# The place of the input's quarter sums on VectorE in a two-layer hybrid decoder trunk

## The chip, the cores and the metric

The kernel runs on one core of a Trainium2 chip. A core has a matrix engine (TensorE, PE in the profile), a vector engine (VectorE, DVE), a scalar engine (ScalarE, ACT), a general engine (GpSimd, POOL) and a queue engine for transfers (SyncE, SP). Each engine works through its own list of instructions in the order in which the list was written; the engines wait for each other by semaphores. The metric is the device time of one execution in microseconds (us), the median of several runs. Less is better.

## The reference

The reference computes a trunk of two layers over one sequence of 512 positions with 2048 features. Each layer normalises its input, multiplies it by one combined input projection and feeds three branches: a short gated convolution, a stick-breaking attention of 8 heads, and a gated linear attention (GLA) of 4 heads. The three results, each times its own gate, are joined and go through an output projection into the residual stream.

```python
def _layer(x, norm_g, w_in, conv_w, conv_b, sb_qn_g, sb_kn_g, gla_w_up, gla_b_up, gla_on_g, w_out):
    h = _rmsnorm(x, norm_g).astype(x.dtype)
    proj = h @ w_in
    ...
    y_conv = _short_conv(cv_h, cv_b, cv_c, conv_w, conv_b) * jax.nn.silu(cv_g.astype(f32))
    q = _rmsnorm(sb_q.reshape(b, s, SB_HEADS, SB_HD), sb_qn_g)
    k = _rmsnorm(sb_k.reshape(b, s, SB_HEADS, SB_HD), sb_kn_g)
    ...
    y_sb = _stick_breaking(q, k, v) * jax.nn.silu(sb_g.astype(f32))
    g = jax.nn.log_sigmoid((gl_lr @ gla_w_up + gla_b_up).astype(f32)) / GLA_TAU
    o = _gla(gl_q, gl_k, gl_v, g)
    y_gla = _rmsnorm(o, gla_on_g).reshape(b, s, GLA_W) * jax.nn.silu(gl_g.astype(f32))
    mix = jnp.concatenate([y_conv, y_sb, y_gla], axis=-1).astype(x.dtype)
    return x + mix @ w_out
```

All data are float32. GLA's queries and keys have 256 columns each, its values and its gate 512 each.

## The kernel before

**Two 16-bit parts for one number.** The kernel multiplies in float16. It writes each float32 operand as a high part (rounded) and a low part (what is left) and takes three of the four cross products. ScalarE makes a high part by a copy with a scale, VectorE the low part by a subtraction. The normalised input lies so in two big tiles `xh` and `xl`, transposed, and stays there for a whole layer.

**Weights.** The weights come in 76 groups of 256 columns, 38 for each layer, in the order in which PE uses them. In a layer the order is: GLA values (two groups, `gla v 0` and `gla v 1`, the second with 16 more columns for the decay's low-rank input), GLA queries (`gla q`), GLA keys (`gla k`), GLA gate (`gla gate 0` and `gla gate 1`), then the convolution's and the attention's groups and the output projection. `fetch` (L362) loads a group two ahead of use on POOL's queue into one of two `st` buffers. `squares` sums its squares on ScalarE (L383), POOL adds them over the partitions (`PARTITION_ALL_REDUCE`, L399), and `wscale` makes a power-of-two scale `ws` of that with four small VectorE steps (L402 to L417). Then `whi` makes the high part of each half of the group on ScalarE (L454) and `wlo` the low part on VectorE (L461), into three buffers each. All of this is traced with a high priority.

**Quick groups.** Most groups, from `gla gate 0` on, are multiplied by a scheme with seven products in place of eight on quarters of the two matrices (`project_quick`, matmuls on L793 and L796). For it a group's weights are split into seven sums of quarters (`wsums`: ScalarE L507, VectorE L508 and the additions L527, L529, L532). The input needs four sums of its quarters as well. `sums_of`, called for the input by `xsums`, makes them once for a layer, in two halves `t` of 256 positions. Each half takes twelve VectorE steps, all recorded on L734 since one helper `do` issues them and keeps them in the list `steps`, and four ScalarE copies (L742). The four parts are written to the tile `s` in float16. The scratch tiles have the tags `zw` and `g`, with two buffers each. `project_quick` first multiplies the first quarter of `x` itself, then parts 0, 2 and 3 of the sums, later part 1.

**Who sets the order.** The code is traced in program order, and a scheduler then writes each engine's list by a simulation of the time: of what is ready it takes what has the highest priority, which is the place in the program, except inside `tc.high_priority`. `order(a, b)` adds an edge without a semaphore: `a` comes behind `b` in the schedule. The kernel uses it to steer. The start of the kernel is laid out by hand for VectorE and ScalarE up to `byhand.__exit__`.

**Around the change.** In a layer the values' groups come first (`project_by_token`, matmuls on L843), then a loop over the tags `qT` and `kT` projects GLA's queries and keys (`project_cols`, L701 to L703) and scales each by its largest entry (`V.tensor_reduce` on L1012 and small steps). Right after the queries, at the end of the loop's first pass, the program calls `xsums`. The decay's work (running sums on L984, its exponent steps L976 to L981) stands ahead of the loop, and in the first layer so does `make_masks` (L134 to L144). Behind the loop stand the two gates and GLA's chunk work (L1044 to L1111), for which POOL clears two tiles of tag `zw` (L1064).

The counter `cursor[0]` counts the groups that have been taken by `weights()`; after the projection of the queries it has moved past them, so that `cursor[0] - 1` is the group `gla q` of that layer.

Of the kernel before, what the change touches and what calls it, by code (L numbers as in the profile page):

```python
# [11 lines left out]
ALU = mybir.AluOpType  # L12
# [31 lines left out]
def hybrid_trunk(ctx, tc, x, norm_g, w_in, conv_w, conv_b, sb_qn_g, sb_kn_g,  # L44
                 gla_w_up, gla_b_up, gla_on_g, w_out, out):
    nc = tc.nc
    V, S, G, T = nc.vector, nc.scalar, nc.gpsimd, nc.tensor
# [5 lines left out]
    GW = 256  # L53
# [21 lines left out]
    def sm(n, tag, bufs=None):  # L75
        return small.tile([P, n], F32, tag=tag, name=nm(tag), bufs=bufs or 1 + (tag in TWICE))

    def wk(shape, tag, bufs=None, dt=F32):
        return work.tile(shape, dt, tag=tag, name=nm(tag), bufs=bufs)

    def newbig(tag, shape, dt, side):
        return big.tile(shape, dt, tag=f"big{side}", name=nm(tag))
# [97 lines left out]
    def allmax(src, n, tag):  # L180

        gm = sm(n, tag + "gm")
        G.partition_all_reduce(gm, src, P, RED.absmax)
        return gm

    def pow2(dst, m, lift, tag):

        c = sm(dst.shape[-1], tag + "pc")
        V.tensor_scalar(c, m, 2.0 ** -90, None, ALU.max)
        V.tensor_scalar(c.bitcast(I32), c.bitcast(I32), 0x7F800000, None, ALU.bitwise_and)  # L190
        V.tensor_scalar(dst, c, 2.0 ** lift, None, ALU.mult)
# [3 lines left out]
    def order(a, b):  # L195
        tc.add_manual_dep(a.ins, b.ins.name, mybir.DependencyInfo(
            mybir.DependencyClass.NoSync, mybir.DependencyReason.DATA), reason="order")
# [145 lines left out]
    loaded = {}  # L343
    cursor = [0]

    staged, whole, narrow, peak, scales = {}, {}, {}, {}, {}

    def junk(n):

# [108 lines left out]

    def wlo(i, h):
        wh, wl = loaded[i][0][h]  # L460
        V.scalar_tensor_tensor(wl[:, :, :GW], staged[i][h], scales[i], wh[:, :, :GW], ALU.mult, ALU.subtract)  # L461
        if i in narrow:
            V.scalar_tensor_tensor(wl[:, :, GW:], narrow[i][:, h * HK:(h + 1) * HK, :], scales[i], wh[:, :, GW:],
                                   ALU.mult, ALU.subtract)
# [12 lines left out]
    def parts_of(i, mm):  # L477

        with tc.high_priority():
            order(wscale(i), mm)  # L480
            if i in quick:
                wsums(i)
                return
            for h in range(2):
                whi(i, h)
                wlo(i, h)
# [165 lines left out]
    xlow(0, 0, mix, True)  # L652
    xlow(0, 1, mix, True)
    wlo(0, 0)
    wlo(0, 1)
    xhigh(1, 0, mix)
    xhigh(1, 1, mix)
# [27 lines left out]
    for l in range(depth):  # L685
# [45 lines left out]
        def sums_of(src, parts, room):  # L731

            def do(f, *a):
                steps.append(f(*a))  # L734

            for t in range(2):
                (h11, h12), (h21, h22), (l11, l12), (l21, l22) = (
                    (a[:, q, 0::2, :], a[:, q, 1::2, :]) for a in src for q in (t, t + 2))

                def put(n, a):  # L740
                    hi, lo = (p_[:, t] for p_ in parts[n])
                    S.activation(hi, a, AF.Copy)  # L742
                    do(V.tensor_tensor, lo, a, hi, ALU.subtract)

                e, g, f = room(t)
                do(V.tensor_tensor, f, h22, l22, ALU.add)
                do(V.tensor_tensor, e, h21, f, ALU.subtract)
                do(V.tensor_tensor, e, e, l21, ALU.add)
                do(V.tensor_tensor, g, h11, e, ALU.subtract)
                do(V.tensor_tensor, g, g, l11, ALU.add)  # L750
                put(0, g)
                do(V.tensor_tensor, f, g, f, ALU.subtract)
                put(3, f)
                put(1, e)
                do(V.tensor_tensor, e, h12, g, ALU.subtract)
                do(V.tensor_tensor, e, e, l12, ALU.add)
                put(2, e)
            return parts
# [11 lines left out]
        def xsums():  # L770

            parts = []
            for _ in range(2):
                a = newbig("s", [P, 4, 2, HK, P], F16, 1 - l)
                parts.extend([a[:, 2 * n], a[:, 2 * n + 1]] for n in range(2))
            return sums_of((xh, xl), parts, lambda t: [wk([P, HK, P], tag) for tag in ("zw", "zw", "g")])
# [47 lines left out]
        def project(cols, dst):  # L824

            if cursor[0] not in quick:
                return project_cols() if cols else project_toks(xh, xl)
            y = dst()
            for _, u in project_quick((xh, xl), insums, y, cols):
                pass  # L830
            if cols:
                return [y[:, c, :] for c in range(2)], u
            return [y[:, 2 * b:2 * b + 2, :].rearrange("p a c -> p (a c)") for b in range(2)], u
# [55 lines left out]
        steps = []  # L889
# [81 lines left out]
        for p in range(2):  # L971
# [3 lines left out]
            a = wk([P, seq], "ga")  # L975
# [26 lines left out]
        for tag in ("qT", "kT"):  # L1002
            o = wk([P, 2, seq], tag)
            ps, u = project(True, lambda: o)
            mx = sm(2, "gamx")
            if tag == "kT":
                with tc.high_priority(offset=1 << 20):
                    for c in range(2):
                        S.activation(o[:, c, :], ps[c], AF.Copy)
                ps = [o[:, c, :] for c in range(2)]  # L1010
            for c in range(2):
                V.tensor_reduce(mx[:, c:c + 1], ps[c], AX.X, ALU.max, apply_absolute_value=True)  # L1012
            gm = allmax(mx, 2, "ga")
            m = sm(1, "gam")
            V.tensor_tensor(m, gm[:, 0:1], gm[:, 1:2], ALU.max)
            p2 = sm(1, tag + "p2")
            pow2(p2, m, -14.0, "ga")
            s_ = sm(1, "gas")
            V.reciprocal(s_, p2)
            for c in range(2):  # L1020
                S.activation(o[:, c, :], ps[c], AF.Copy, scale=s_)
            qk.append(o)
            un = sm(1, tag + "un")
            V.tensor_tensor(un, p2, u, ALU.mult)
            qku.append(un)
            if tag == "qT":
                insums = xsums()
        gq, gk = qk
        att_u = sm(1, "attu")
        V.tensor_scalar(att_u, qku[0], qku[1], 0.125, ALU.mult, ALU.mult)  # L1030
# [289 lines left out]
        for j in range(4):  # L1320
# [21 lines left out]
            for n in range(2):  # L1342
# [11 lines left out]
                for b in range(2):  # L1354
# [4 lines left out]
                    for i in range(4):  # L1359
                        cs = slice(i * P, (i + 1) * P)  # L1360
                        a = S.activation(e[:, cs], rb.rearrange("p a c -> p (a c)")[:, cs], AF.Square,
                                         accum_out=sq[:, 8 * n + 4 * b + i:8 * n + 4 * b + i + 1])
# [42 lines left out]
        steps, out_ = [], {}  # L1405
# [74 lines left out]
```

## Time and profile before

| what | value |
|---|---|
| median of 3 runs | 1647.73 us (1642.52 to 1655.6) |
| the profiled execution | 1646.43 us |
| its span in the profile | 1644.6 us |
| granted TensorE clock | 1.00 |
| data moved | 235.97 MB, 143 GB/s mean |
| GLA queries on PE, first layer | from 74.07 us |
| GLA gate 0 on PE, first layer | from 117.66 us |
| GLA gate 0 on PE, second layer | from 924.43 us |

How to read the profile: the page gives the busy time of each engine, the waits and the groups of instructions by line. A row of the timeline has the start in us, the duration in us, the engine, the line, the operation and its tiles (written `out<-in`), the number of instructions merged into the row, and in brackets how long the engine had been idle before it and what ended that. Durations of neighbouring VectorE rows overlap by about 0.1 us, so the time that a step takes from its engine is the distance between starts. A row of the waits has the engine and the waiting instruction, the releasing one, the sum in us, how often, and the longest. The view by stretch gives each engine's busy time with the number of its instructions in brackets. `wl` and `wh` are low and high parts of weights, `s` the input's sums, `x` or `m` the input's own parts (the first and the second layer), `psp` an accumulator of PE.

### The profile page before, as it was taken

The numbers are of one execution on the slowest core, as the hardware profiler recorded it, in microseconds if no ns is written. First come the engines' busy times: TensorE is split into PE (matmuls) and PEld (weight loads), VectorE is DVE, ScalarE is ACT, GpSimd is POOL, SyncE is SP. The second block draws the span as 40 slices with busy tenths as digits, with TensorE's granted clock in tenths as the row PEclk, the third lists the DMA queues.
The fourth block names the chain that finished last, engine by engine and source line by source line (L and its number), as shares of the span: only waits on it lengthen the run. The fifth ranks groups of instructions, "written<-read, shape, count | busy, mean of one in ns | idle before, by whom it ended". The sixth has DMA issues, their size and how long they took to land.

```text
span 1644.6 us, 41938 instructions
## 1 busy us (share of the span) xinstructions
PE 1619.6 (98%) x18058; PEld 1356.1 (82%) x18058; DVE 1433.7 (87%) x2403; ACT 1192.3 (72%) x1763; POOL 270.7 (16%) x300
## 2 busy tenths in 40 slices
PE   8999999999999999999999999999999999999999
PEld 5757768989899967799986668689898989768998
DVE  7989989989898979898699899898988889878893
ACT  7668887977777776756766788788777878666571
POOL 0122021211112121111102111211121212110110
PEclk9999999999999999999999999999999999999999
DMA  7154435477868677544643544546776776894441
GB/s 260 54 129 140 93 118 114 108 160 142 166 149 167 149 167 197 171 155 142 203 120 105 129 116 116 140 83 140 151 157 153 158 158 155 174 196 141 155 155 53
DMA packets 195995, 235.97 MB, mean 143 GB/s; under 512 B 90259, under 2 KB 156125, under 8 KB 195297
## 3 DMA queue, kind: packets, MB, share of 16 engines
q0 software_dynamic: 79072, 178.27, 41.2%
q1 hardware_dynamic: 107728, 45.56, 14.6%
q10 hardware_dynamic: 9008, 9.45, 1.8%
q8 instruction: 141, 2.31, 0.6%
q14 instruction: 46, 0.37, 0.1%
HBM read 179.65 MB, written 14.68 MB: 118 GB/s over the span
## 4 chain that ended last, share of the span: by engine, by line
PE 33%; DVE 10%; ACT 4%; DMA 3%; issue 2%; SPq 0%; POOL 0%; DVEq 0%; ACTq 0%; POOLq 0%
PE psp L796 11%; PE psp L793 6%; PE psp L843 4%; PE psp L714 2%; PE psp L713 2%; PE psp L712 2%; DVE wl L508 2%; PE psp L702 1%; PE psp L701 1%; PE psp L703 1%; DMA m<-mixd 1%; ACT wh L507 1%; ACT junk L383 1%; DMA kT<-raw 1%; DVE wl L461 1%
## 5 line engine op out<-in xcount | busy, mean ns | idle before, releaser
L507 ACT ACTIVATE wh<-st,ws 128x1024 f16<-128x1024 f32 x264 | 293.8, 1144 | 168.3 <-DVE st L527 89.8
L508 DVE SCALAR_TENSOR_TENSOR wl<-st,ws,wh 128x1024 f16<-128x1024 f32 x264 | 332.1, 1280 | 24.0 <-ACT wh L507 23.8
L383 ACT ACTIVATE junk<-st 128x2048 uint8<-128x2048 f32 x150 | 285.5, 1903 | 19.4 <-DMA st<-in_w_out_dram 10.4
L793 PE MATMUL psp<-s,wh 128*128 128x256 f16 x1280 | 217.7, 273 | 0.0
L793 PEld LDWEIGHTS <-wh 128*128 128x128 f16 x1920 | 187.4, 98 | 23.4 <-issue 1.4
L796 PE MATMUL psp<-wh,s 128*128 128x128 f16 x2048 | 177.2, 219 | 0.8 <-issue 0.8
L714 PE MATMUL psp<-wh,m 128*128 128x256 f16 x640 | 174.5, 273 | 3.1 <-DVE m L1195 3.1
L793 PE MATMUL psp<-s,wl 128*128 128x256 f16 x640 | 174.3, 273 | 0.9 <-DVE wl L508 0.9
L712 PE MATMUL psp<-wh,m 128*128 128x256 f16 x640 | 174.5, 273 | 0.0
L713 PE MATMUL psp<-wl,m 128*128 128x256 f16 x640 | 174.5, 273 | 0.0
L796 PEld LDWEIGHTS <-s 128*128 128x128 f16 x3072 | 172.9, 98 | 1.2 <-issue 1.2
L796 PE MATMUL psp<-wl,s 128*128 128x128 f16 x1024 | 173.3, 219 | 0.0
L461 DVE SCALAR_TENSOR_TENSOR wl<-st,ws,wh 128x2048 f16<-128x2048 f32 x64 | 149.4, 2347 | 16.2 <-ACT wh L454 15.6
L362 POOL DMA_DIRECT2D st<-in_w_in_dram x114 | 110.9, 1051 | 256.0 <-DVE w7l L508 112.7
L454 ACT ACTIVATE wh<-st,ws 128x2048 f16<-128x2048 f32 x62 | 122.4, 1995 | 32.3 <-DVE ws L415 19.2
L796 PEld LDWEIGHTS <-m 128*128 128x128 f16 x2304 | 131.0, 98 | 2.5 <-issue 2.1
L399 POOL PARTITION_ALL_REDUCE wgm<-wm x75 | 55.6, 742 | 456.9 <-ACT junk L383 442.8
L386 POOL DMA_DIRECT2D st<-st x36 | 57.3, 1591 | 356.0 <-ACT junk L383 336.7
L793 PEld LDWEIGHTS <-wl 128*128 128x128 f16 x960 | 93.9, 98 | 13.2 <-DVE wl L508 1.4
L796 PE MATMUL psp<-wh,m 128*128 128x128 f16 x1024 | 91.5, 219 | 0.7 <-DVE ws L415 0.4
L796 PE MATMUL psp<-wl,m 128*128 128x128 f16 x512 | 87.5, 219 | 0.0
L843 PEld LDWEIGHTS <-m 128*128 128x128 f16 x768 | 75.0, 98 | 12.4 <-DMA m<-th 1.3
(443 smaller groups left out, 4136.8 us busy)
## 6 DMA issues: line engine op xcount, KB each, us to landing
st<-in_w_in_dram POOLq DMA_DIRECT2D x114, 1024.0 KB, 8.4
st<-in_w_out_dram POOLq DMA_DIRECT2D x32, 1024.0 KB, 9.3
st<-st POOLq DMA_DIRECT2D x36, 512.0 KB, 6.7
st<-in_w_in_dram SPq DMA_DIRECT2D x6, 1024.0 KB, 12.0
mixd<-g POOLq DMA_DIRECT2D x20, 256.0 KB, 8.0
x<-in_x_dram SPq DMA_DIRECT2D x4, 1024.0 KB, 4.9
qT<-in_x_dram ACTq DMA_DIRECT2D x8, 512.0 KB, 6.8
qT<-xs ACTq DMA_DIRECT2D x8, 512.0 KB, 4.0
```

The costliest lines, as they stand in the source:

```text
L362: load = queue.dma_start(s_, src[l, h * HK * P:(h + 1) * HK * P, c0:c0 + GW].rearrange("(k p) n -> p k n", p=P), max_dma_last_dim=1024)
L383: sq = S.activation(junk(HK * GW).rearrange("p (k n) -> p k n", k=part.shape[1]), part, AF.Square, accum_out=peak[i][:, h:h + 1])
L454: hi = S.activation(wh[:, :, :GW], staged[i][h], AF.Copy, scale=scales[i])
L461: V.scalar_tensor_tensor(wl[:, :, :GW], staged[i][h], scales[i], wh[:, :, :GW], ALU.mult, ALU.subtract)
L507: hi = S.activation(h_, b, AF.Copy, scale=sc)
L508: V.scalar_tensor_tensor(l_, b, sc, h_, ALU.mult, ALU.subtract)
L712: T.matmul(o, ah[:, t, k, :], wh[:, kk, :n], start=st_, stop=False, skip_group_check=True)
L713: T.matmul(o, ah[:, t, k, :], wl[:, kk, :n], start=False, stop=False, skip_group_check=True)
L714: return T.matmul(o, al[:, t, k, :], wh[:, kk, :n], start=False, stop=en, skip_group_check=True)
L793: mm = T.matmul(o, w[q_][:, kk, :], a[p_][:, :, kk, :], start=st_, stop=en, skip_group_check=True)
L796: mm = T.matmul(o[:, t * P:(t + 1) * P], a[p_][:, t, kk, :], w[q_][:, kk, :], start=st_, stop=en, skip_group_check=True)
L843: mm = T.matmul(o[:, :n], a_[:, t, k, :], w[k // HK][part][:, k % HK, :n], start=i == 0 and k == 0, stop=i == 2 and k == KT - 1)
```

## The change

`wlo` keeps its last VectorE instruction for each group in a new dictionary `lows`; as it is called for the two halves of a group in turn, what stays is the low part of the second half. After `xsums`, all 24 VectorE steps of the sums are ordered behind the low part of the second half of `gla q`. The list `steps` is set up anew in each layer, so it holds the sums of that layer alone at this place. The edge has no semaphore and works within VectorE; ScalarE's copies follow by their data. Nothing is computed in another way.

```diff
-    staged, whole, narrow, peak, scales = {}, {}, {}, {}, {}
+    staged, whole, narrow, peak, scales, lows = {}, {}, {}, {}, {}, {}
...
     def wlo(i, h):
         wh, wl = loaded[i][0][h]
-        V.scalar_tensor_tensor(wl[:, :, :GW], staged[i][h], scales[i], wh[:, :, :GW], ALU.mult, ALU.subtract)
+        lows[i] = V.scalar_tensor_tensor(wl[:, :, :GW], staged[i][h], scales[i], wh[:, :, :GW], ALU.mult, ALU.subtract)
         if i in narrow:
...
             if tag == "qT":
                 insums = xsums()
+                for a in steps:
+                    order(a, lows[cursor[0] - 1])
         gq, gk = qk
```

## The prediction

> **What bounds the kernel now.** I read the head of the page first, then the waits of TensorE (PE), then the busy time of each engine by stretch around the edit, then VectorE's (DVE) and PE's timeline there.
>
> ```profile
> span 1644.6 us, 41938 instructions
> PE 1619.6 (98%) x18058; PEld 1356.1 (82%) x18058; DVE 1433.7 (87%) x2403; ACT 1192.3 (72%) x1763; POOL 270.7 (16%) x300
> ```
>
> PE is idle for 1644.6 - 1619.6 = 25.0 us of the whole span. No change of order on DVE can give more than that, and 1% (about what a measurement of this kernel can tell from no change) is 16.5 us. Where does PE wait near the edit? These are its waits between 40 and 121 us; between 852 and 927 us, the same place in the second layer, the view has none.
>
> ```profile
> PE psp L703 <- DVE wl L461: 1.3, 1, 1.3
> PE psp L843 <- ACT wh L456: 0.6, 1, 0.6
> PE psp L843 <- DVE kpc L190: 0.6, 1, 0.6
> ```
>
> The busy time by stretch (columns: stretch, its length, then busy us and instruction count of PE, weight loads, DVE, ACT, POOL, then granted clock, DMA share, GB/s):
>
> ```profile
> 40.00:76.00 36.00, 33.40 (x289) 28.03 (x287) 35.74 (x64) 25.26 (x32) 4.84 (x5) 1.00 0.20 62
> 852.00:885.00 33.00, 33.00 (x281) 27.32 (x280) 32.97 (x44) 22.01 (x26) 2.61 (x4) 1.00 0.21 67
> 80.57:122.79 42.22, 42.22 (x223) 21.49 (x222) 34.96 (x81) 27.80 (x33) 12.46 (x12) 1.00 0.54 125
> 884.47:929.56 45.09, 45.09 (x237) 22.80 (x236) 35.57 (x74) 31.04 (x37) 13.15 (x12) 1.00 0.51 117
> 120.28:240.00 119.72, 119.28 (x1074) 87.20 (x1072) 110.53 (x205) 98.53 (x149) 18.46 (x21) 1.00 0.43 119
> 927.05:1040.00 112.95, 112.51 (x1043) 84.14 (x1041) 103.73 (x195) 94.15 (x143) 18.44 (x21) 1.00 0.46 126
> ```
>
> In the first two rows DVE is full; PE is idle 2.6 us in the first layer and not at all in the second. In the next two, where the edit sends work, DVE has 42.22 - 34.96 = 7.3 us and 45.09 - 35.57 = 9.5 us free. PE binds everywhere here; DVE matters only where PE must wait for it.
>
> **What the change moves.** Nothing is added or removed. Each layer has 24 VectorE steps of the input's sums (all on L734; 12 for each of two halves). Those that stand ahead of the last low part of the query weights must now stand behind it. The sums' busy time ahead of that low part, and the rows of DVE that mark the places:
>
> ```profile
> 40.00:78.30 38.30, 23.77 (x20) 1.00 0.19 58
> 852.00:882.20 30.20, 20.05 (x17) 1.00 0.23 73
> ...
> 44.53 1.22 DVE L734 TENSOR_TENSOR zw<-x,zw 128x1024 f32<-128x1024 f16 x1
> 46.98 0.14 DVE L190 TENSOR_SCALAR kpc<-kpc 128x1 int32<-128x1 int32 x1
> 71.11 1.21 DVE L734 TENSOR_TENSOR s<-zw,s 128x1024 f16<-128x1024 f32 x1
> 72.25 1.21 DVE L734 TENSOR_TENSOR zw<-zw,x 128x1024 f32<-128x1024 f32 x1
> 73.60 2.33 DVE L461 SCALAR_TENSOR_TENSOR wl<-st,ws,wh 128x2048 f16<-128x2048 f32 x1
> 78.30 2.33 DVE L461 SCALAR_TENSOR_TENSOR wl<-st,ws,wh 128x2048 f16<-128x2048 f32 x1
> 882.21 2.33 DVE L461 SCALAR_TENSOR_TENSOR wl<-st,ws,wh 128x2048 f16<-128x2048 f32 x1
> ```
>
> So 20 of 24 steps move in the first layer (their tie is the low part at 78.30) and 17 in the second (882.21). Start to start a step takes 72.25 - 71.11 = 1.14 us: 22.8 us and 19.4 us of DVE work. The ACT copies that feed the low halves of the sums (L742) go with them; ACT has over 14 us free in each receiving stretch, so I cost them at nothing; were ACT full they would delay the sums one for one.
>
> **What it can give.** In the first layer the low part at 73.60 starts late because DVE is full, and PE waits for it:
>
> ```profile
> 69.94 3.88 ACT L454 ACTIVATE wh<-st,ws 128x2048 f16<-128x2048 f32 x2
> ...
> 75.99 0.39 PE L703 MATMUL psp<-x,wl 128*128 128x512 f16 x1 [1.32 <-DVE wl L461]
> ```
>
> Both high parts lie between 69.94 and 73.82. With DVE free the low parts can run at about 71.9 and 74.2 and be done by 76.5 rather than 80.57, 4.1 us sooner, and the 1.3 us go. The wait of 0.6 us for L190 is behind sums on DVE too (44.53 ahead of 46.98 above), so I count it: 1.9 us. The 0.6 us for the ACT high part is the open one: from 0 (its scale is late for another reason) to 0.6. Gain 1.3 to 2.6 us, taken as 1.9. What is late next there is PE itself. The second layer gives 0, since PE has no wait to lose.
>
> On this bound a rule of the Trainium skill can be weighed. It says (Perfetto Trace Analysis, Identifying the Most-Contended Engine) that matmul busy time is no measure of how near TensorE is to its limit, and that the weight-load share is. By weight loads the stretch from 40 to 76 us has 36.00 - 28.03 = 8.0 us of room, and with a gain of that size the sum below would be about 1642.5 us; by the idle rows it is at most 2.6 us. I go by idle time, because a matmul stream without gaps can't be made denser by another order on DVE.
>
> **What it can cost.** The sums have a last moment. The first gate projection of the linear attention reads them; PE runs its first product from x, then three products of 24 matmuls each from s:
>
> ```profile
> 120.28 0.27 PE L793 MATMUL psp<-s,wh 128*128 128x256 f16 x1
> 128.14 0.27 PE L793 MATMUL psp<-x,wh 128*128 128x256 f16 x1
> 927.05 0.27 PE L793 MATMUL psp<-s,wh 128*128 128x256 f16 x1
> ```
>
> (128.14 - 120.28) / 3 = 2.62 us a product. The second of them reads part 2, whose low half is the last step of all: it must be there by 122.9 us and 929.7 us. Up to there 22.8 us must go into 7.3 us of free DVE time in the first layer, and 19.4 into 9.5 in the second: 15.5 and 9.9 us too much, if nothing gives way. What gives way, from these rows:
>
> ```profile
> 85.98 0.31 DVE L962 CAST qT<-lr 128x48 bf16<-128x48 f32 x2
> 87.66 0.29 DVE L962 CAST qT<-lr 128x32 bf16<-128x32 f32 x2
> 92.18 0.69 DVE L969 CAST e<-psm 128x512 bf16<-128x512 f32 x1 [0.58 <-PE psm L965]
> 96.46 2.93 DVE L141 TENSOR_SCALAR masks<-e 128x256 uint8<-128x256 f32 x7
> 102.75 0.42 DVE L1078 TENSOR_TENSOR e<-raw 128x256 f32<-128x256 f32 x1
> 107.03 0.76 DVE L1087 SCALAR_TENSOR_TENSOR e<-e,qT 128x256 f32<-128x256 f32 x2 [1.41 <-ACT qT L1021]
> 108.74 0.75 DVE L1050 TENSOR_TENSOR th<-e,th 128x256 f16<-128x256 f32 x2
> 110.69 0.66 DVE L1012 TENSOR_REDUCE gamx<-kT 128x1 f32<-128x512 f32 x1
> 118.62 4.87 DVE L508 SCALAR_TENSOR_TENSOR wl<-st,ws,wh 128x1024 f16<-128x1024 f32 x4 [1.17 <-ACT wh L507]
> ```
>
> First, the start 4.1 us sooner (first layer only). Second, the chunk work of the linear attention, which the code emits after the sums: L1078 and L1079 (four of about 0.34 from start to start), L1087, L1050, L1012, together about 3.4 us. Third, the small steps of the decay's low-rank input, which the sums delay today: six groups between 85.98 and 87.66, about 1.6 us, can run sooner. Left are 15.5 - 9.1 = 6.4 us and 9.9 - 5.0 = 4.9 us. Fourth, of the four low parts at 118.62 only the first is needed before 122.9, so up to 3 x 1.2 = 3.6 us can give way, though the code gives weights the higher priority: 2.8 and 1.3 us. The masks (2.93 us) could also move into the emptied stretch, which would bring the first layer to 0; but they begin right behind the cast at 92.18, and I leave them there. So PE's new wait is 0 to 6.4 us in the first layer and 1.3 to 4.9 in the second. I take 2.8 and 1.3, the ends where the weights' later low parts yield, because the rows show DVE gaps just ahead of them that wait for ACT (1.17 us at 118.62), in which a sum step fits.
>
> Queues: the moved steps stand on DVE and ACT alone, but POOL clears two zw tiles that the sums held:
>
> ```profile
> 86.13 0.95 POOL L1064 MEMSET zw<- 128x1024 f32 x1 [0.50 <-DVE s L734]
> L1092 DVE COPY_PREDICATED zw<-masks,psz x28: 687/727/1316, 141.9 to 1083.3; 128x512 f32<-128x512 uint8 x28
> ```
>
> They will come some 35 us later; the first reader is at 141.9, so there are about 20 us to spare, and I cost them at nothing. Behind them on POOL stand weight loads and scale reductions; if a memset blocked those, the next gate's weights would be late.
>
> **The sum**, against the profiled execution's own 1646.4 us: -1.9 + 2.8 + 1.3 = +2.2, so 1648.6 us. The median of the runs shown is 1.3 us above that execution, well inside the runs' spread of 13 us. Its own range goes from -2.6 (no new wait) to 6.4 + 4.9 - 1.3 = +10.0: 1643.8 to 1656.4.
>
> **The rivals.**
> (a) No new wait: the sums fit, the old waits go. 1646.4 - 2.6 = 1643.8 us. For it: DVE has gaps and the low-priority work is real. Against it: 9.9 us must be found in the second layer, where the start can't come sooner.
> (b) The other side: the sums are plainly late, nothing gives way, and PE stands at the second product from s in each layer: 15.5 + 9.9 - 1.3 = +24.1, 1670.5 us. It decides (over 16.5) when less than 7.6 us of the 25.4 give way in both layers together. For it: priorities are fixed in the code, and weights' parts go first. Against it: 3.4 us a layer are emitted after the sums.
> (c) The debt is carried on: the work that gave way (3.4 + 3.6 us a layer) holds up the chunk work and the evictions behind 120 and 927 us. DVE has 119.72 - 110.53 = 9.2 us free there, and 9.2 in the second layer, so it should fit; if none of it were usable: 2.2 + 14.0 = +16.2, 1662.6 us.
> (d) A long stall slows PE's clock. At the start, after an idle stretch, PE took 3.57 us for eight 512-column matmuls, where 0.2157 each is the pace later:
>
> ```profile
> 6.06 3.57 PE L244 MATMUL psz<-qp,identb 4*128 4x512 bf16 x8
> 76.22 0.38 PE L701 MATMUL psp<-x,wh 128*128 128x512 f16 x1
> 76.43 0.38 PE L702 MATMUL psp<-x,wh 128*128 128x512 f16 x1
> ```
>
> That is 1.84 us lost. If both layers stalled by their upper ends and paid it again: 6.4 + 4.9 + 3.7 - 1.3 = +13.7, 1660.1 us. Against it: the granted clock reads 1.00 in every stretch above, and a stall that long needs the upper ends. The Trainium skill's page TensorE: Matmul & The Clock Gate (What you observe; What's actually happening) has such a rule: an idle window of about 3.4 us sends the array to half speed. No PE wait in the rows above is that long, so this trace can't confirm the threshold.
> (e) Much faster. It would take 16.5 of the 25.0 us of PE's idle time, of which 2.6 lie here; only another order far downstream could do it.
>
> **How the numbers follow.** Forecast 0.50; (a) 0.27; (b) 0.08; (c) 0.06, half of it over 1%; (d) 0.05, of which 0.01 over; (e) 0.04. Faster by over 1%: 0.04. Slower: 0.08 + 0.03 + 0.01 = 0.12. Within 1%: 0.84. The range leaves out (b) and most of (e), and adds the runs' spread of some 5 us below (a): 1639 to 1663, the upper end being (c).
>
> **What would show it.** Right: L734 begins at about 76 and 884 us, not 40 and 852; the wait of 1.3 us at the query projection is gone; the first s product in the gate comes later than PE could start it, with a wait of 1 to 3 us put down to L734 or L742. Wrong: a wait of over 5 us there, a clock under 1.00 behind it, PE waits between 130 and 240 us that are not there now, or the sums spread out past the gate. The forecast falls if PE's total idle time changes by more than 10 us.

## The result and the profile after

| | before | after |
|---|---|---|
| median | 1645.73 us (4 runs) | 1665.47 us (1662.69 to 1672.44, 4 runs) |
| profiled execution | 1646.43 us | 1662.69 us |
| span in the profile | 1644.6 us | 1660.9 us |

After to before is 1.0131, with a 95% interval of [1.0098, 1.0163]: slower, 16.9 us above the forecast of 1648.6 us and just outside its range. Ratios in this document leave out the few executions that ran in a slower state (5908.36 us in e11_load8 is one); medians count them.

The head of the page of the changed kernel:

```profile
span 1660.9 us, 41951 instructions
PE 1623.1 (98%) x18058; PEld 1357.5 (82%) x18058; DVE 1434.6 (86%) x2403; ACT 1194.7 (72%) x1763; POOL 273.1 (16%) x300
```

TensorE's (PE) waits over the whole of this run begin with:

```profile
PE psp L793 <- ACT wh L507: 6.7, 3, 3.6
PE psp L793 <- DVE wl L508: 6.1, 5, 2.7
```

VectorE (DVE) has as much work as before (1434.6 against 1433.7 us). PE is idle for 1660.9 - 1623.1 = 37.8 us, 12.8 more than before, and busy 3.5 us longer with the same 18058 matmuls, so some of them ran slower. These two waits are for high and low parts of quarter weights. PE has no wait for the sums (L734, L742) anywhere. PE's timeline at the two places (line numbers below L1027 are two higher than in the kernel before):

```profile
115.70 0.27 PE L793 MATMUL psp<-x,wh 128*128 128x256 f16 x1 [0.36 <-ACT qT L1021]
...
118.32 0.27 PE L793 MATMUL psp<-s,wh 128*128 128x256 f16 x1
...
124.70 0.40 PE L793 MATMUL psp<-s,wh 128*128 128x256 f16 x1 [3.60 <-ACT wh L507]
125.90 0.39 PE L793 MATMUL psp<-s,wh 128*128 128x256 f16 x1 [0.80 <-ACT wh L507]
128.38 0.39 PE L793 MATMUL psp<-s,wl 128*128 128x256 f16 x1 [2.09 <-DVE wl L508]
...
134.93 0.27 PE L793 MATMUL psp<-x,wh 128*128 128x256 f16 x1
...
934.90 0.27 PE L793 MATMUL psp<-s,wh 128*128 128x256 f16 x1
...
940.28 0.28 PE L793 MATMUL psp<-s,wh 128*128 128x256 f16 x1 [2.35 <-ACT wh L507]
943.29 0.40 PE L793 MATMUL psp<-s,wl 128*128 128x256 f16 x1 [2.73 <-DVE wl L508]
...
950.27 0.27 PE L793 MATMUL psp<-m,wh 128*128 128x256 f16 x1
```

Gate 0 of the first layer starts at 115.70 us where it started at 117.66: 1.96 us gained. Then the three products from the sums take 134.93 - 118.32 = 16.61 us. Before they took 128.14 - 120.28 = 7.86. In the second layer they take 950.27 - 934.90 = 15.37, where 7.86 (934.91 - 927.05) was the time before. That is 8.75 and 7.51 us lost, 16.26 together. That the whole span is 16.3 us longer is a chance agreement: the gain and several smaller shifts elsewhere nearly cancel. This duration of the three products is the measure used below.

The waits are 3.60 + 0.80 + 2.09 = 6.49 us of the 8.75, and 2.35 + 2.73 = 5.08 of the 7.51. Of the other 2.3 and 2.4 us, the clock makes some 1.5 and 2.0: the 15 matmuls from 128.38 to 131.55 us take 3.17 us, where 15 x 0.109 = 1.64 us is their pace before, and the 19 from 943.29 to 947.32 us take 4.03 in place of 2.07. The rest is how a wait is counted, namely from the end of the matmul before it, which comes 0.27 us or more after its start, while matmuls otherwise start 0.109 us apart. By single microseconds (stretch, length, busy us and count of PE, weight loads, DVE, ACT, POOL, then granted clock, DMA share, GB/s):

```profile
124.00:125.00 1.00, 0.30 (x1) 0.10 (x1) 1.00 (x3) 0.95 (x2) 0.94 (x1) 0.85 0.41 46
125.00:126.00 1.00, 0.20 (x2) 0.10 (x1) 1.00 (x2) 0.84 (x1) 0.50 (x1) 0.50 0.00 0
...
130.00:131.00 1.00, 1.00 (x7) 0.69 (x6) 1.00 (x2) 0.00 (x0) 0.00 (x0) 0.50 0.00 0
131.00:132.00 1.00, 1.00 (x9) 0.78 (x8) 1.00 (x9) 0.00 (x0) 0.91 (x1) 0.74 0.00 0
```

Behind the wait of 3.60 us the granted clock drops to 0.50 and stays there until about 131.5 us; 6 or 7 matmuls run in a microsecond in place of 12. The Trainium skill (TensorE: Matmul & The Clock Gate; What's actually happening) has the clock halved after an idle window of about 3.4 us, with the window running freely; by that rule a wait of 3.6 us is enough where it holds a whole window, and the trace agrees.

Why were the weight parts late? VectorE's timeline at the place, first after, then before:

```profile
116.09 1.22 DVE L734 TENSOR_TENSOR s<-zw,s 128x1024 f16<-128x1024 f32 x1
117.23 1.37 DVE L984 TENSOR_TENSOR_SCAN raw<-ones,ga 128x128 f32<-128x128 f32 x4
118.51 0.40 DVE L1080 TENSOR_TENSOR e<-raw 128x256 f32<-128x256 f32 x1
...
119.83 1.22 DVE L527 TENSOR_TENSOR st<-st 128x1024 f32<-128x1024 f32 x1
...
123.44 1.22 DVE L529 TENSOR_TENSOR st<-st 128x1024 f32<-128x1024 f32 x1
```

```profile
114.97 1.22 DVE L527 TENSOR_TENSOR st<-st 128x1024 f32<-128x1024 f32 x1
116.23 1.22 DVE L529 TENSOR_TENSOR st<-st 128x1024 f32<-128x1024 f32 x1
```

The last step of the sums is done by 117.3 us, ahead of the first product that reads them (118.32). But the addition L527, whose high part PE waits for at 124.70, stands behind that step, four running sums and two exponent differences of the chunk work (L1080, L1081, each twice), and comes 4.9 us later than before; L529 comes 7.2 us later. ScalarE's list adds to the first wait. L527 is done at 121.05 us, but ScalarE makes the high part of it only at 123.50, behind a sum of squares for a later group and two exponents of the chunk work:

```profile
120.57 1.91 ACT L383 ACTIVATE junk<-st 128x2048 uint8<-128x2048 f32 x1
122.46 1.14 ACT L1082 ACTIVATE e<-e 128x512 f32<-128x512 f32 x2
123.50 2.34 ACT L507 ACTIVATE wh<-st,ws 128x1024 f16<-128x1024 f32 x2
```

So some 2.4 of the 3.60 us pass on ScalarE; no run here changes its order alone. In the second layer it is not so: there ScalarE stands idle for 0.87 us until L529 is done (939.04 us), and makes the high part at once. VectorE by stretch, before and then after:

```profile
40.00:74.00 34.00, 32.73 (x286) 27.86 (x285) 33.74 (x63) 23.26 (x30) 4.84 (x5) 1.00 0.21 65
74.00:118.00 44.00, 42.68 (x205) 19.47 (x203) 37.36 (x82) 29.50 (x36) 12.35 (x12) 1.00 0.41 108
118.00:130.00 12.00, 12.00 (x113) 10.75 (x110) 10.95 (x22) 8.79 (x11) 2.82 (x4) 1.00 0.40 45
```

```profile
40.00:74.00 34.00, 34.00 (x295) 28.63 (x293) 21.16 (x55) 20.08 (x28) 3.17 (x5) 1.00 0.21 65
74.00:118.00 44.00, 42.52 (x209) 20.09 (x208) 43.77 (x75) 27.65 (x31) 10.28 (x10) 1.00 0.40 108
118.00:130.00 12.00, 5.51 (x39) 3.93 (x37) 12.00 (x20) 9.55 (x14) 5.99 (x4) 0.78 0.41 45
```

The tie leaves VectorE 12.6 us (33.74 - 21.16) idler ahead of 74 us. From there to 118 it can win back 6.4 (43.77 - 37.36) and is then full. At 118 us, where PE comes to the sums, VectorE has done 33.74 + 37.36 = 71.10 us of work before the change and 64.93 after: it is 6.2 us behind.

### The profile page after: what moved, and what is told of

Same layout as the page of the kernel before. It is cut to its first block, busy times and chain, and to the rows that moved or that the text cites. A ratio compares the mean times of both kernels' runs of the same rounds, so it can differ in the third digit from the quotient of the medians.

```text
span 1660.9 us, 41951 instructions
## 1 busy us (share of the span) xinstructions
PE 1623.1 (98%) x18058; PEld 1357.5 (82%) x18058; DVE 1434.6 (86%) x2403; ACT 1194.7 (72%) x1763; POOL 273.1 (16%) x300
## 4 chain that ended last, share of the span: by engine, by line
PE 38%; DVE 8%; ACT 2%; issue 2%; DMA 1%; POOL 0%; DVEq 0%; ACTq 0%; POOLq 0%
PE psp L796 12%; PE psp L793 7%; PE psp L843 4%; PE psp L712 3%; PE psp L713 3%; PE psp L714 3%; DVE wl L508 2%; PE psp L702 1%; PE psp L701 1%; PE psp L703 1%; DVE wl L461 1%; PE psm L1312 1%; DVE zw L734 1%; ACT junk L383 1%; PE psz L1272 1%
## 5 line engine op out<-in xcount | busy, mean ns | idle before, releaser
L508 DVE SCALAR_TENSOR_TENSOR wl<-st,ws,wh 128x1024 f16<-128x1024 f32 x264 | 332.2, 1281 | 21.5 <-ACT wh L507 21.4
L383 ACT ACTIVATE junk<-st 128x2048 uint8<-128x2048 f32 x150 | 285.7, 1905 | 21.1 <-DMA st<-in_w_in_dram 12.6
L793 PE MATMUL psp<-s,wh 128*128 128x256 f16 x1280 | 221.7, 275 | 7.7 <-ACT wh L507 6.7
L796 PEld LDWEIGHTS <-m 128*128 128x128 f16 x2304 | 131.0, 98 | 1.7 <-issue 1.1
L386 POOL DMA_DIRECT2D st<-st x36 | 57.2, 1589 | 305.7 <-ACT junk L383 261.4
```

The source lines that it names most:

```text
L383: sq = S.activation(junk(HK * GW).rearrange("p (k n) -> p k n", k=part.shape[1]), part, AF.Square, accum_out=peak[i][:, h:h + 1])
L508: V.scalar_tensor_tensor(l_, b, sc, h_, ALU.mult, ALU.subtract)
L793: mm = T.matmul(o, w[q_][:, kk, :], a[p_][:, :, kk, :], start=st_, stop=en, skip_group_check=True)
L796: mm = T.matmul(o[:, t * P:(t + 1) * P], a[p_][:, t, kk, :], w[q_][:, kk, :], start=st_, stop=en, skip_group_check=True)
```

## The experiments

The expectations speak of theories by letters. A: PE waits for gate 0's weight parts, which stand behind pushed-back work in VectorE's list. B: PE waits for the sums themselves, which are late. C: the second layer's loss is carried over from the first. D: any tie upsets the written order downstream. E: VectorE has too much to do there, and another order only moves the wait. The "load theory" of the last four is E put as a dose: work beyond what VectorE has time for makes PE wait, whoever reads it. The results together. Each ratio is taken to the kernel before as it ran beside that kernel: its median was 1646.03 us beside e1, e2, e4 and e5, 1643.09 beside e6, e10, e8 and e3, and 1642.06 beside the last four. The products are read from the one profiled execution of each kernel, which can lie off the median: 1681.18 us for e8_v4, 1684.66 for e12_load20, 1671.29 for e6_weights, 1661.22 for e5_scans.

| kernel | median, us | ratio to before, 95% | three products, layer 1 | layer 2 |
|---|---|---|---|---|
| before | 1645.73 | | 7.86 us | 7.86 us |
| the change | 1665.47 | 1.0131 [1.0098, 1.0163] | 16.61 | 15.37 |
| e1_first | 1651.89 | 1.0038 [1.0015, 1.0060] | 16.95 | 7.86 |
| e2_second | 1653.88 | 1.0046 [1.0022, 1.0070] | 7.86 | 15.70 |
| e4_values | 1649.77 | 1.0023 [0.9992, 1.0055] | 13.42 | 12.73 |
| e5_scans | 1655.74 | 1.0048 [1.0023, 1.0072] | 17.07 | 12.11 |
| e6_weights | 1664.42 | 1.0126 [1.0093, 1.0159] | 11.01 | 9.80 |
| e10_order | 1655.48 | 1.0075 [1.0056, 1.0094] | 12.85 | 9.92 |
| e8_v4 | 1664.08 | 1.0153 [1.0114, 1.0192] | 7.86 | 7.86 |
| e3_half | 1642.50 | 0.9994 [0.9966, 1.0022] | 7.86 | 7.86 |
| e13_dose | 1653.78 | 1.0066 [1.0043, 1.0088] | 11.73 | 12.65 |
| e7_keys | 1673.84 | 1.0179 [1.0141, 1.0218] | 17.96 | 16.91 |
| e11_load8 | 1660.91 | 1.0103 [1.0065, 1.0140] | 14.21 | 9.97 |
| e12_load20 | 1675.66 | 1.0201 [1.0158, 1.0244] | 17.79 | 12.32 |

**One layer at a time.**

```diff
-                for a in steps:
+                for a in steps if l == 0 else ():      # e1_first
+                for a in steps if l else ():           # e2_second
```

> The tie in the first layer only. Theory A (work pushed back on VectorE stands ahead of the gate's weight parts, the additions L527 and L529 and the low parts L508, and PE waits for those at GLA gate 0): the first layer keeps its gain of about 4 us before the gate and its loss of about 13 us at it, and the second layer goes as before: about 9 us over the kernel before. Theory B (the loss is the sums' own lateness): the same total, but with PE's wait put down to L734 or L742. Theory C (the loss in the two layers hangs together, one delay carried on): the whole 16 to 20 us stay with one tie.

> The tie in the second layer only. Theory A: nothing to gain ahead of the gate there, about 11 us lost at gate 0 and 1 of the second layer, so about 11 us over the kernel before. Theory B: the same total with the wait at the sums. Theory C: less than 4 us, if the first layer's delay is the root.

Each layer pays for itself, though with 5.9 and 7.9 us by the medians it pays less than the 9 and 11 that were expected. With the first alone its products take 16.95 us and the second layer's 7.86; with the second alone it is 7.86 and 15.70. The ratios add up (0.38% and 0.46%) to less than the whole change's 1.31%, so something is left over that depends on the whole schedule. One place of that kind lies far behind: at the second layer's output projection PE waits 3.1 us for VectorE's scaling of the joined results in the kernel before (L1195) and 3.2 in e2_second, but not at all in e1_first and in the change. Neither profile has a wait for the sums, so B falls too. That the second layer's loss is carried over from the first (C) falls.

**The same tie, one group sooner.**

```diff
-                    order(a, lows[cursor[0] - 1])
+                    order(a, lows[cursor[0] - 2])
```

> The sums tied one group earlier, behind the last low part of the second values' group, in both layers. They can then begin some 20 us sooner than in the changed kernel, in the first layer at about 51 us, and fill the stretch that the change left empty. Theory A: the first layer's gain of 2 to 4 us stays, since the input's own low parts and the first weights still go ahead of the sums, no wait above 1 us comes at gate 0, and the time is 0 to 5 us under the kernel before. Theory D (any tie upsets the written order downstream): still 8 us or more over it.

Gate 0 starts at 113.83 us, 3.8 sooner than before, and one wait is left in each layer. Theory A expected none above 1 us and a time up to 5 us under the kernel before; the waits are 2.81 and 2.80 us, and the time cannot be told from it (ratio 1.0023, interval from 0.9992). What was not expected is how much a wait costs: 2.81 us of it make the three products of the first layer 13.42 - 7.86 = 5.56 us longer. PE's timeline there, then single microseconds as above:

```profile
124.99 0.40 PE L793 MATMUL psp<-s,wl 128*128 128x256 f16 x1 [2.81 <-DVE wl L508]
```

```profile
124.00:125.00 1.00, 0.01 (x1) 0.01 (x1) 1.00 (x2) 0.00 (x0) 0.00 (x1) 0.56 0.00 0
...
130.00:131.00 1.00, 1.00 (x7) 0.69 (x6) 0.31 (x2) 0.82 (x1) 0.00 (x0) 0.52 1.07 422
```

The clock is half from about 124.1 to 131.0 us. The 23 matmuls from 124.99 to 129.87 us take 4.88 us in place of 2.51, so the clock costs nearly as much as the wait that set it off.

**Another order behind the same tie.** Four kernels change what stands ahead of gate 0's weight parts. e5_scans puts the decay's running sums behind L529. e10_order leaves those alone and puts the parts for gate 0's later products behind the one that its third product from the sums reads (both engines), and the last quarter addition (L532) too. e6_weights does that and puts L981, L984 and the keys' maxima behind that part too. e8_v4 takes the sooner tie of e4_values with the order of e10_order, and moves the second half of L981 and L984 and the second maximum.

```diff
+        for a in late:                      # e5_scans: the running sums
+            order(a, adds[cursor[0]])
...
+            if names[i] == "gla gate 0" and n > 3:     # e10_order, e6_weights, e8_v4
+                order(hi, ends[i, 3][0])
+                order(lo, ends[i, 3][1])
...
+        for a in late:                      # e6_weights, e8_v4: L981, L984, L1012
+            order(a, ends[cursor[0], 3][1])
```

> The changed kernel, with the decay's running sums (L984) and so all of the chunk work behind them ordered behind the second quarter addition (L529) of gate 0's weights, in both layers. The load of VectorE is the same, only its order differs. Theory A: the additions and low parts come some 4 us sooner, PE's waits at gate 0 fall from over 6 us a layer to under 3, the clock stays at 1.00, and the time is 8 to 14 us under the changed kernel, that is within 1% of the kernel before. Theory E (VectorE has too much to do there whatever the order): PE waits elsewhere between 120 and 240 us and the time stays within 4 us of the changed kernel.

> The changed kernel, but in both layers the decay's additions and running sums, the scaling maxima of the keys and the last quarter addition stand on VectorE behind the low part of gate 0's weights that its third product from the sums reads, and the parts for the later products stand behind that one on both engines. Theory A (PE waits for gate 0's weight parts because pushed-back work stands ahead of them in VectorE's list; the sums themselves are in time): PE's waits at gate 0 fall from 6.5 us to at most 3 us in the first layer and likewise in the second, none as long as 3 us, the granted clock stays near 1.00 there, and the median is 1644 to 1653. Theory E (VectorE has too much work in the stretch whatever its order): the work that is now put behind the weights makes PE wait or the lag grow between 130 and 200 us and between 950 and 1000 us, and the median stays at 1658 or more.

> The changed kernel; only the order among gate 0's own weight parts is set right (the parts for the later products and the last quarter addition behind the low part for the third product from the sums, on ScalarE and VectorE), the running sums and chunk work stay ahead. If the loss comes from the weight parts' own order, the median is 1652 or less; if it comes from the pushed-back work ahead of all of them (theory A in its narrow form), PE still waits some 3 to 4 us for the first addition's high part in the first layer, only the wait of 2.1 us behind it goes, and the median is 1658 to 1664. Theory E: 1663 or more.

> The kernel with the sums tied one group sooner (behind the last low part of the second value group), and gate 0's weight parts in the order in which PE reads them, with the second half of the decay's sums, the keys' second maximum and the last quarter addition behind the third of them. Theory A: the single wait of 2.8 us in each layer falls to at most 1.2 us, the granted clock stays 1.00, the gain of 3.9 us ahead of the first gate is kept through 240 us, and the median is 1640 to 1645, ratio to the kernel before 0.995 to 0.9995. Theory E: the time comes back behind the gate and the median is 1648 or more.

By their ratios e5_scans and e10_order lose less than the change, so the order in the list is a part of the loss. Both miss what was expected all the same. In e5_scans the first layer's waits are 1.82 + 0.76 + 4.04 = 6.62 us, not under 3; only the second layer's fall, to 2.45. e10_order, at 1655.48 us, lies between the two ranges that it was to tell apart. e6_weights and e8_v4 are misses that teach most. At the three products they do what was wanted: 11.01 us in e6_weights, of which 2.99 us are a wait behind the last of them, and 7.86 us in e8_v4 without any wait. Yet they end as slow as the change. Behind those products, PE's timeline in e6_weights, and its waits over the whole run in e8_v4 (PE's quick matmuls are on L799 in both, an eviction of their accumulator on L815):

```profile
128.65 0.37 PE L799 MATMUL psp<-x,wh 128*128 128x256 f16 x1 [2.99 <-DVE g L815]
145.91 0.45 PE L1070 MATMUL psz<-th,qp 64*128 64x64 f16 x8 [2.08 <-ACT qp L1056]
```

```profile
PE psp L799 <- DVE wl L508: 12.9, 6, 3.6
PE psp L720 <- DVE m L1212: 11.4, 2, 6.4
```

In e6_weights the wait has moved to the eviction of an accumulator and to the chunk work, which is E. In e8_v4 the fourth product waits 2.60 us for its low part (at 126.43 us), 12.9 us in all are waits for such low parts, and 11.4 us are lost where the joined results are scaled for the output projection (L1212), far from any edit. That last wait is not one for work on VectorE: VectorE itself stands idle there for 14.2 us until a read of the joined results from memory (`m<-mixd`) has landed. In the second layer that read lands 30.4 us after its issue, 18.5 in the kernel before and 13.0 in the change. e6_weights has the same wait, 8.4 us for PE with a read of 24.3 us, so a part of what these two profiles lose says nothing about E. What holds the read up stays open. VectorE's work by 118 us in e8_v4 is 33.02 + 36.73 = 69.75 us, only 1.4 behind the kernel before, so load alone doesn't explain that kernel; beyond the read, why it falls so far back was not settled.

**The dose.** Fewer steps tied, or the same steps tied later:

```diff
-                for a in steps:
+                for a in steps[12:]:       # e3_half; steps[6:] in e13_dose
...
-                    order(a, lows[cursor[0] - 1])
+                    order(a, lows[cursor[0]])          # e7_keys
```

> Only the twelve steps of the second half of the sums are tied, in both layers, so 8 steps in the first layer and 5 in the second are moved in place of 20 and 17: 9.1 and 5.7 us of VectorE work, against 7.3 and 9.5 us that it had free ahead of the gate. Theory A: little work is pushed behind, PE's waits at gate 0 are under 2 us in each layer, the clock stays 1.00, median 1643 to 1650. A rival (any move brings the whole loss, because the scheduler's list changes as a whole): 1658 or more.

> All but the first six steps of the sums are tied, in both layers: 14 and 11 steps moved (16 and 12.5 us) where the kernel with half of them moves 8 and 5 and the changed kernel 20 and 17. Load theory, on the line between those two (loss at the gates 0 and 12 us a layer): 4 to 8 us a layer in the first, 2 to 6 in the second, median 1645 to 1656. Rival (all or nothing): 1643 or 1663.

> The changed kernel with the tie one group later, behind the last low part of the key weights (some 10 to 13 us later). Load theory: VectorE stands emptier ahead of it and is full for longer behind it, so the loss grows to 18 to 30 us a layer and now PE also waits for the sums themselves, median 1675 to 1705. Rival (the gate's weight parts alone, the loss does not grow with the delay): 1660 to 1670.

| kernel | steps moved, layers 1 and 2 | VectorE's work, 40 to 118 us | three products, layer 1 |
|---|---|---|---|
| before | 0, 0 | 33.74 + 37.36 = 71.10 us | 7.86 us |
| e3_half | 8, 5 | 30.94 + 40.17 = 71.11 | 7.86 |
| e13_dose | 14, 11 | 25.29 + 42.18 = 67.47 | 11.73 |
| the change | 20, 17 | 21.16 + 43.77 = 64.93 | 16.61 |
| e7_keys | 24, 24 | 21.63 + 40.87 = 62.50 | 17.96, begun 5.35 us late |

Ratio and dose go together: 13, 25, 37 and 48 moved steps give -0.06, +0.66, +1.31 and +1.79%. With e3_half, VectorE has done by 118 us exactly what it had done before, and PE shows no wait over 0.4 us at the gate. Its rows:

```profile
40.00:74.00 34.00, 32.72 (x286) 27.78 (x284) 30.94 (x67) 22.34 (x29) 3.70 (x5) 1.00 0.21 65
74.00:118.00 44.00, 44.00 (x216) 20.95 (x215) 40.17 (x79) 31.50 (x39) 10.65 (x12) 1.00 0.45 114
```

e13_dose falls within what was expected for the time; e7_keys, at 1673.84 us, just under it, with 15.5 and 15.2 us lost at the gates in place of 18 to 30. Only in e7_keys do the sums themselves come too late. Its waits at gate 0 of the first layer have the names that the prediction looked for in the change:

```profile
PE psp L793 <- ACT s L742: 5.3, 1, 5.3
PE psp L793 <- DVE wl L508: 4.3, 1, 4.3
PE psp L793 <- DVE s L734: 1.9, 1, 1.9
```

**Load that nobody reads.** The sums stay where they were; maxima over the input that nothing uses are added at the place to which the change moves the sums.

```diff
-                for a in steps:
-                    order(a, lows[cursor[0] - 1])
+                idle = sm(2 * NT, "own")[:, 0:1]
+                for n in range(17 if l else 20):       # 8 and 8 in e11_load8
+                    a = V.tensor_reduce(idle, xh[:, n % 4, :HK, :].rearrange("p k c -> p (k c)"), AX.X, ALU.max)
+                    order(a, lows[cursor[0] - 1])
```

> The sums are not tied. In their place 8 maxima over 1024 entries of the input's high part are added in each layer, ordered behind the same low part of the query weights; nothing reads them. Estimated from the 0.66 us of a maximum over 512 entries at some 1.2 us each: 9.6 us more VectorE work, against 7.3 and 9.5 us that it has free ahead of the gate. Load theory (VectorE has no more than that free, and any work beyond it makes PE wait, whoever reads it): PE's loss at gate 0 is 0 to 3 us in each layer, median 1643 to 1652. Rival (the loss of the change comes from PE having to wait for what the sums feed): no loss, 1640 to 1648. This dose alone tells little apart, the next kernel does.

> As the kernel with 8 maxima, but with 20 in the first layer and 17 in the second, as many as the change moves steps: some 24 and 20 us of VectorE work that nothing reads. Load theory: VectorE is full from 80 to 130 us and from 885 to 935 us as in the changed kernel, PE waits at gate 0 for weight parts, the granted clock falls there, and the loss is 8 to 16 us in each layer, median 1658 to 1680. Rival (the sums' own lateness): median 1640 to 1650.

The group of the added instructions in e12_load20's first layer (count, busy us, mean ns), then its stretches:

```profile
L1030 DVE TENSOR_REDUCE own<-x 128x1 f32<-128x1024 f16 x20 | 24.1, 1205 | 0.0
```

```profile
74.00:118.00 44.00, 41.98 (x196) 18.98 (x197) 43.97 (x81) 23.67 (x27) 8.86 (x11) 1.00 0.41 108
118.00:130.00 12.00, 6.00 (x51) 4.77 (x49) 12.00 (x20) 8.33 (x12) 3.17 (x3) 0.92 0.40 45
```

In the first layer the picture is that of the change: VectorE full, PE half idle from 118 to 130 us, the clock below 1.00, the three products at 17.79 us, with the longest wait (6.02 us) for a low part of gate 0's weights (L508). In the second they take 12.32 us, and this profile too has 10.5 us of waits at the output projection. No sum was moved. So the sums need not be late, nor need PE wait for them: work on VectorE at this place is enough. e11_load8 missed its range (1643 to 1652): 19.2 us of useless work (16 x 1.2) cost some 17 us by its ratio (11 to 23 by the interval), though VectorE had 7.3 and 9.5 us free in the two stretches. From 74 to 118 us VectorE is busy for 39.12 us, only 1.76 more than in the kernel before, though 8 x 1.2 = 9.6 us were added there. A likely reading is that its idle time is scattered waiting for other engines, and that an added step seldom falls into it without pushing something that PE needs.

## Why the prediction was wrong, step by step

- **The bound** held: PE's stream sets the time, and all of the loss is PE standing or running at half clock.
- **The start** held: the sums begin at 73.64 us in the first layer (said: about 76). **The gain** came out right in part by luck. Gate 0 begins 1.96 us sooner (said: 1.9), but that is a larger gain less a cost that the sum lacks: all three waits go, the queries begin 2.10 us sooner (71.97 us) and run through, and then PE waits 1.12 us for the keys' copy out of an accumulator (L1009) and 0.36 us at the gate (L1021). The second layer has such a wait of 1.0 us as well, where the sum has nothing.
- **The excess** was somewhat smaller than said. The 6.4 us of the first layer leave out the 3.4 us of chunk work that was to give way, so the forecast's lag of VectorE in all is 9.8 us; measured are 6.2 us at 118 us and 75.38 - 69.83 = 5.6 at 122.9 us. For the second layer the step said 4.9 + 3.4 = 8.3; with that layer alone tied, VectorE's work from 852 to 926 us falls from 64.44 us to 14.04 + 43.80 = 57.84, which is 6.6.
- **The step that failed** is the fourth relief and what hung on it: weights keep their priority, only their later low parts yield, and PE's new wait is 2.8 and 1.3 us for the sums. The sums were in time. The weights were late, and the early ones: the two additions L527 and L529 and the parts made of them, on VectorE and, for one wait of the first layer, on ScalarE as well. The lists show decay and chunk work ahead of them, so a priority in the code doesn't say what comes first in a list that is already full; that the scheduler's simulation thought these parts not yet ready there is a reading of the lists and was not tried by itself. PE's waits were 6.49 and 5.08 us, not 2.8 and 1.3.
- **The last moment** was misread too. PE takes the product with the last part of the sums (part 2) first of the three, at 118.32 us, not second: it is the only one of them whose weights need neither L527 nor L529, which are not done by then. This did no harm here.
- **The clock**, rival (d), happened in both layers and was given 0.05. Its price, said to be 1.84 us a layer, held nearly: 1.5 and 2.0 us. Its condition did not. The step held that it needs a stall at the upper end, 6.4 and 4.9 us in one; a stall of 3.60 us was enough in the first layer, and one of 2.35 us in the second.
- **The plainly late sums**, rival (b), gave 1670.5 us, near the time, but for another reason. Its mechanism is that of e7_keys.
- **The debt carried on**, rival (c), is not seen in the change: the lag behind the first gate is 134.93 - 128.14 = 6.8 us, and the second layer's first matmul of the values comes at 818.87 in place of 811.70 us, 7.2 later. It is what e6_weights shows.
- **POOL's clears**, put at nothing, cost nothing that shows. They come at 110.19 and 117.38 us in place of 84.61 and 86.13, and the transfer behind them on POOL (L386) is issued at 118.42 in place of 115.81 us; PE's waits between 131 and 240 us are 1.9 us in all.
- **The sum** that was measured: -1.96 + 8.75 + 7.51 = +14.3 us, and some 2 us of shifts along the way, against the +2.2 forecast. The medians stand 19.7 us apart, the profiled spans 16.3; the difference is spread between runs.

## What to carry to other kernels

Before work is moved to a later place on an engine that is full nearly everywhere, count the idle time that the move leaves behind: that much must be won back before the next due point, and here some 6 us in each layer that were not won back cost 16 us together. Idle time in the receiving stretch need not be room, since it can be scattered waiting, and what comes late need not be the moved work: here it was what the engine's list put last. Count with the half clock behind a stall of the matrix engine of two microseconds or more: at the three places where it was worked out here it cost 1.5 to 2.4 us.

## What the runs showed of the hardware

Waits well below 3.4 us halved the clock as well: 2.81 us in e4_values, where the clock fell some 1.9 us after the last matmul before the wait had ended (122.2 to 124.1 us), and 2.35 us in the second layer of the change, where the clock reads 0.74 from 940 to 941 us and 0.50 from there. In the first layer of e13_dose two waits of 1.09 and 0.77 us close together (until 124.76 and 125.81 us) did it, and the clock fell when PE had been running again for 1.1 us:

```profile
127.00:128.00 1.00, 1.00 (x7) 0.72 (x6) 1.00 (x2) 0.00 (x0) 0.00 (x0) 0.52 0.00 0
```

By the rule of the Trainium skill cited above, an idle window has to be some 3.4 us long; these windows were not idle throughout, so the measurement goes further than the rule.

The length of the wait does not decide alone. A wait of 2.74 us in the change (until 1314.37 us) left the clock at 1.00. At the output projection two waits of 1.04 and 2.06 us left it at 1.00 in the kernel before, while 1.09 and 2.12 us at the same place in e2_second halved it. What else decides was not tested.

Half clock lasted about 6.8 us in the change (124.7 to 131.5) and in the first layer of e4_values (124.1 to 131.0), but 3.4 us in the second layer of e4_values (936.5 to 939.9) and in e13_dose (127.0 to 130.5). The matmuls of 256 columns then started 0.214 us apart in place of 0.109. A half clock that spans a second wait costs little there, since PE stands anyway; behind the last wait it costs the full factor until it ends.
